# Two of four weight sums per seven-product block moved from VectorE to adding transfers issued from GpSimd, in a two-layer hybrid decoder trunk

## The chip, the cores and the metric

The kernel runs on one core of a Trainium2 chip. A core has five engines that run side by side, each with its own queue: TensorE (PE in the profile; PEld is its loading of weights), VectorE (DVE), ScalarE (ACT), GpSimd (POOL) and SyncE (SP, which here only issues transfers). Waiting is done at the head of an engine's queue, so an instruction that waits holds back all that stand behind it on that engine. The metric is the device time of one execution in microseconds (us).

## The reference, cut to what matters

Two layers of a decoder trunk over 528 positions (16 learned ones and 512 real ones), width 1024. Each layer is an attention part and a feed-forward part:

```python
hn = rmsnorm(h, ffn_norm_g)
ff = jax.nn.silu(jnp.einsum('bld,df->blf', hn, w_gate)) * jnp.einsum('bld,df->blf', hn, w_up)
return h + jnp.einsum('blf,fd->bld', ff, w_down)
```

The change touches only the first two products, with `w_gate` and `w_up`, each 1024 x 2816 in float32. All is held transposed: a tile has 128 features in its partitions and the positions along its free dimension.

## The kernel before

**Products in three parts.** To keep float32 accuracy, each operand is split into a high part (a cast to float32r on ScalarE) and a low part (the rest, by a subtraction on VectorE). A product is then three matmuls: high by high, high by low, low by high. For weights this split is `splits` (line 887: the cast at line 888, the subtraction at line 889); its results lie in two rings of weight buffers, `whi`/`wlo` and `fwhi`/`fwlo`, two buffers each, and successive weight jobs alternate between the rings. A new job's split so waits until TensorE is through with the job four places before it.

**Seven products for eight.** The inner dimension of 1024 is eight blocks of 128. For 19 of the 22 blocks of 128 hidden features (a `Unit`, line 907, f = 3 to 21), gate and up are taken together as a 2 x 2 block product, by a scheme with seven block products in place of eight. It needs sums of weight blocks and sums of input blocks. The input sums are made once per layer by `x_forms` (line 854): four calls, each filling a scratch tile `S` of six parts (lines 861 to 865) and splitting four of them into `th` and `tl`. The weight sums are made per unit: `a` is the block of `w_gate` (tile `raw`, tag with three buffers, shared with the `w_down` loads), `b` the block of `w_up` (tile `fraw`, two buffers), and `s` a further tile with tag `S`, of which there are two buffers in all, shared by `x_forms` and the units. The four sums are those of lines 934, 935, 941 and 947, all on VectorE, each 128 x 512.

**Jobs of a unit.** `make1` splits `a` itself, `make2` builds `s` (lines 934 and 935) and splits it, `make3` overwrites the first half of `b` (line 941) and splits `b`, `make4` overwrites the second half of `a` (line 947) and splits that half. `load` (line 920) issues the two transfers of 512 KB from SyncE. TensorE runs, per unit, `head` (job 1), `middle` (jobs 2 and 3), a group of `w_down` products (line 1035, `down`), `tail` (the rest of job 3, and job 4), and a second group of `down`. `keep` (line 961) and `done` (line 972) bring results out of PSUM: copies at line 966 on ScalarE, sums at lines 969 and 976 on VectorE, then SiLU and the gated product. The first three blocks of hidden features run as plain products (lines 206 and 828 to 849), and during them the four calls of `x_forms` are placed (lines 1236 and 1237).

**Order.** Only TensorE's instructions run in the order written (line 1349). On the other engines the framework sets the order, together with the buffers: an instruction may stand well ahead of its place in the text if it has nothing to wait for. It is fixed when the program is built. The layers share memory: the feed-forward stage's tiles lie on the bytes of the attention stage's tiles and each waits for the users of its own bytes. The next attention stage's first memsets (line 85) are issued from GpSimd in layer 1.

The split of the weights and the loop that calls it ahead:

```python
def need(j):
    for i in range(j, min(j + 3, len(jobs))):
        if i <= j or "make" in jobs[i]:
            convert(i)
```

Of the kernel before, what the change touches and what calls it, by code (L numbers as in the profile page):

```python
# [10 lines left out]
F32 = mybir.dt.float32  # L11
F32R = mybir.dt.float32r
AF = mybir.ActivationFunctionType
ALU = mybir.AluOpType

D = 1024
NK = D // 128
# [3 lines left out]
DEPTH = 2  # L21
# [7 lines left out]
HB = NK // 2  # L29
# [10 lines left out]
def hybrid_kernel(ctx, tc, x_t, w_in, w_fl, w_out, w_gate, w_up, w_down, vecs, b_fg, rope, decay, mask, ident, out_t):  # L40
    nc = tc.nc

    const = ctx.enter_context(tc.tile_pool(name="const", bufs=1))
# [11 lines left out]
    vec = const.tile([128, vecs.shape[1]], F32, name="vec")  # L55
# [70 lines left out]
    def vcol(c):  # L126
        return vec[:, c:c + 1]


    def split(hi, lo, src, pinned=False):  # L130
        pin(nc.scalar.copy(hi, src), pinned)
        pin(nc.vector.tensor_sub(lo, src, hi.bitcast(F32)), pinned)
# [122 lines left out]
    def tt(name, dt=F32):  # L255
        tag, bufs = tags[name]
        return tmp.tile([128, T], dt, name=name, tag=tag, bufs=bufs)
# [4 lines left out]
    def fft(tag, dt=F32R, shape=(128, T), bufs=None):  # L262
        return phase["ffn"].tile(list(shape), dt, name=tag, tag=tag, bufs=bufs)
# [28 lines left out]
    RSC = -1.0 / (2.0 * D)  # L292
# [50 lines left out]
    V_ATTN, V_FFN, V_FIN, V_GN = 0, 2 * NK, 4 * NK, 5 * NK  # L343
# [51 lines left out]
    def silu(t, then=None):  # L395
        nc.scalar.activation(t, t, AF.Silu)
        if then:
            tc.keep_in_program_order(nc.scalar.preload_act_table_set(then))
# [414 lines left out]
    def ffn(l, st, real, last):  # L813
# [8 lines left out]
        def two(t):  # L822
            return t[:, t0:T].rearrange("p (a b) -> p a b", a=2)

        def act_tile(f):
            return fft(f"ah{f % 8}"), fft(f"al{f % 8}")
# [27 lines left out]
        def x_forms(k):  # L854
            def go():
                if k == 0:
                    st["t"] = [[fft(f"t{p}{i}", shape=(128, 2, 4, w)) for p in "hl"] for i in range(2)]
                s = fft("S", F32, (128, 6, w), 2)
                a, b = ((h[k][:, c0:c1], h[HB + k][:, c0:c1]) for c0, c1 in HC)
                g0, g1 = vcol(V_FFN + l * NK + k), vcol(V_FFN + l * NK + HB + k)  # L860
                nc.scalar.activation(s[:, 0:2], two(h[k]), AF.Copy, scale=g0)
                nc.vector.tensor_sub(s[:, 2], s[:, 1], s[:, 0])
                for i in range(2):
                    nc.vector.scalar_tensor_tensor(s[:, 3 + i], b[1], g1, s[:, 1 + i], ALU.mult, ALU.subtract)
                nc.vector.scalar_tensor_tensor(s[:, 5], a[1], g1, s[:, 4], ALU.mult, ALU.subtract)
                th, tl = (t[:, k % 2] for t in st["t"][k // 2])
                split(th, tl, s[:, 2:6])
            return go
# [18 lines left out]
        def splits(hi, lo, src):  # L887
            nc.scalar.copy(hi, src)  # L888
            nc.vector.tensor_sub(lo, src, hi.bitcast(F32))  # L889

        def product(j, o, x, bank, fresh, final, n=HB, done=None):

            def chunk(k):
                def go():
                    if k == 0:
                        need(j)
                    _, hi, lo = jobs[j]["w"][0]
                    xh, xl = x(k)
                    for i, (a, b) in enumerate(((hi, xh), (hi, xl), (lo, xh))):
                        nc.tensor.matmul(bank()[:, 0:b.shape[-1]], a[:, o + k, :], b, start=(fresh and k == 0 and i == 0),  # L900
                                         stop=(k == n - 1 and i == 2), skip_group_check=not (fresh and final))
                    if k == n - 1 and done:
                        done()
                return go
            return [chunk(k) for k in range(n)]

        class Unit:
# [12 lines left out]
            def load(self):  # L920
                if "a" not in self.t:
                    for n, src, pool, tag, bufs in (("a", w_gate, wp, "raw", 3), ("b", w_up, phase["ffn"], "fraw", 2)):
                        self.t[n] = pool.tile([128, NK, 128], F32, name=tag, tag=tag, bufs=bufs)
                        nc.sync.dma_start(self.t[n], src[l, self.f])


            def make1(self, hi, lo):
# [1 line left out]


            def make2(self, hi, lo):
                a, b = self.t["a"], self.t["b"]
                s = self.t["s"] = fft("S", F32, (128, NK, 128), 2)
                nc.vector.tensor_add(s[:, HB:NK], b[:, 0:HB], b[:, HB:NK])
                nc.vector.tensor_sub(s[:, 0:HB], s[:, HB:NK], a[:, 0:HB])
                splits(hi, lo, s)


            def make3(self, hi, lo):
                a, b = self.t["a"], self.t["b"]  # L940
                nc.vector.tensor_sub(b[:, 0:HB], a[:, 0:HB], b[:, 0:HB])
                splits(hi, lo, b)


            def make4(self, hi, lo):
                a, s = self.t["a"], self.t["s"]
                nc.vector.tensor_sub(a[:, HB:NK], a[:, HB:NK], s[:, 0:HB])
                splits(hi, lo, a[:, HB:NK])

            def bank(self, n):  # L950
# [21 lines left out]
            def done(self):  # L972
                e = self.t["e"]
                sg = tt("sg")
                with tc.high_priority():
                    nc.vector.tensor_add(two(sg), self.t["zy"][:, :, 0:w], e[:, 0:2])
                c = slice(t0, T)
                nc.vector.scalar_tensor_tensor(sg[:, c], sg[:, c], RSC, st["R"][:, c], ALU.mult, ALU.mult)
                silu(sg[:, c], None if self.f < NF - 1 else ROOTS if last else LOGS)
                u = tt("tq")  # L980
                nc.vector.scalar_tensor_tensor(u[:, c], sg[:, c], RSC, st["R"][:, c], ALU.mult, ALU.mult)
                u2 = two(u)
                nc.vector.tensor_mul(u2[:, 0], self.t["x"][:, 0:w], u2[:, 0])
                nc.vector.tensor_mul(u2[:, 1], e[:, 2], u2[:, 1])
                fh, fl = act_tile(self.f)
                split(fh[:, c], fl[:, c], u[:, c])
                acts[self.f] = (fh, fl)
# [17 lines left out]
        def down_job(p, f0, f1):  # L1005

            n = f1 - f0
            t = {}

            def load():  # L1010
                if t:
                    return
                t["r"] = wp.tile([128, NK, 128], F32, name="raw", tag="raw", bufs=3)
                for s in range(2):
                    nc.sync.dma_start(t["r"][:, s * n:s * n + n], w_down[l, 2 * p + s, :, f0:f1])

            return add_job(load=load, make=lambda hi, lo: splits(hi, lo, t["r"][:, 0:2 * n]), n=2 * n)
# [31 lines left out]
        for r, (f0, f1) in enumerate(ROUNDS):  # L1049
            for f in range(f0, f1):  # L1050
# [4 lines left out]
                u = Unit(f)  # L1055
# [7 lines left out]
                if fills:  # L1063
                    p, g0, g1 = fills.pop(0)
# [175 lines left out]
        steps.insert(4, lambda: squares(st, QC, False, False))  # L1240
        return steps

    gf = const.tile([128, NK], F32, name="gf")
    nc.vector.tensor_scalar_mul(gf, vec[:, V_FIN:V_FIN + NK], RSC)

    def layer(l):
# [79 lines left out]
        for g in range(2):  # L1326
# [15 lines left out]
                      ret_places(3, 52, 45.5, 47.5, 57.5, 55.5, 58.5, 60, 64.1, 63, 64.2))  # L1342
        plan += [op[3], op[7], op[11], op[15]] + op[16:]
        up = ffn(l, ff, real, real)
        plan += [lambda: enter("ffn"), start_ffn] + up
        return plan
# [77 lines left out]
```

## Time and profile before

| | |
|---|---|
| Median of 3 runs | 1272.61 us (1271.99 to 1272.77) |
| The profiled execution's own time | 1272.43 us |
| Its span | 1270.6 us |
| PE busy | 1253.3 us |
| DVE busy | 998.6 us |
| ACT busy | 687.3 us |
| POOL busy | 266.9 us |
| Granted clock of TensorE, mean | 0.999 |
| Transferred | 120.57 MB, mean 95 GB/s |

The profile shows one execution of the program. Times on its time line count from the start of the span. A group's row gives line, engine, operation, result <- operands, shape and count, then busy time and mean duration in ns, then the idle time of the engine before these instructions and what ended it. A row of the time line gives start, duration, engine, line and operation, and in brackets the idle time ahead of it with its releaser. A row of the waits gives total, number and longest. Transfers have a time from issue to landing.

### The profile page before, as it was taken

What the parts mean: (1) busy time and instruction counts of PE and PEld (TensorE: products, weight loads), DVE (VectorE), ACT (ScalarE), POOL (GpSimd) and SP (SyncE); (2) the same over time, 40 slices, a digit from 0 to 9 for tenths busy, and PEclk for the clock granted to TensorE, in tenths of its full rate; (3) what the DMA queues carried; (4) which work ended last, traced back from release to release, by engine and by line L of the source; (5) the groups of instructions that cost most, each with busy time, mean ns of one, the idle gap of its engine ahead of it and who ended that gap; (6) DMA issues with size and microseconds to landing.
All of it is one profiled execution on the core that took longest, in us unless ns stands there. A gap on an engine that the chain in (4) does not pass through costs nothing.

```text
span 1270.6 us, 23600 instructions
## 1 busy us (share of the span) xinstructions
PE 1253.3 (99%) x9263; PEld 1195.1 (94%) x9263; DVE 998.6 (79%) x1852; ACT 687.3 (54%) x1246; POOL 266.9 (21%) x527
## 2 busy tenths in 40 slices
PE   9999999999999999999999999999999999999997
PEld 8899999999999999999998989998789999999996
DVE  8878756779888888887786877567899888888866
ACT  7666545676444444444465665456764444444444
POOL 3455545410000000000025546454100000000000
PEclk9999999999999999999999999999999999999999
DMA  6322222123233333332323232222233333333321
GB/s 217 95 71 89 87 81 83 60 68 129 92 96 100 100 100 100 100 100 84 107 70 117 61 101 83 78 90 67 100 96 121 100 100 100 100 100 100 102 81 67
DMA packets 45680, 120.57 MB, mean 95 GB/s; under 512 B 5360, under 2 KB 12272, under 8 KB 45568
## 3 DMA queue, kind: packets, MB, share of 16 engines
q1 hardware_dynamic: 45136, 118.77, 29.7%
q8 instruction: 73, 1.20, 0.4%
q14 instruction: 39, 0.32, 0.1%
q10 hardware_dynamic: 432, 0.29, 0.1%
HBM read 116.91 MB, written 2.13 MB: 94 GB/s over the span
## 4 chain that ended last, share of the span: by engine, by line
PE 93%; DVE 2%; ACT 2%; DMA 2%; issue 0%; SPq 0%; DVEq 0%; ACTq 0%
PE psd L206 29%; PE psa L900 19%; PE psd L1035 14%; PE psd L900 13%; PE psa L206 5%; PE psa L1035 4%; PE psa L407 2%; PE psa L582 2%; PE psa L497 2%; PE psa L749 1%; PE psa L719 1%; DMA bc<-cdr 1%; DMA h<-x_t 0%; DMA cdr<-z 0%; PE psa L279 0%
## 5 line engine op out<-in xcount | busy, mean ns | idle before, releaser
L183 POOL TENSOR_TENSOR wlo<-raw,whi 128x128 fp32r<-128x128 f32 x504 | 261.4, 554 | 270.0 <-ACT whi L180 250.0
L206 PE MATMUL psd<-xh,whi 128*128 128x264 f32 (+1 forms) x792 | 195.4, 314 | 0.2 <-ACT whi L180 0.2
L206 PE MATMUL psd<-xl,whi 128*128 128x264 f32 (+1 forms) x792 | 186.0, 302 | 0.5 <-DVE xl L309 0.4
L206 PE MATMUL psd<-xh,wlo 128*128 128x264 f32 (+1 forms) x792 | 186.4, 303 | 0.0
L206 PEld LDWEIGHTS psd<-xh,whi 128*128 128x128 f32 x792 | 128.0, 189 | 5.2 <-ACT whi L180 0.9
L206 PEld LDWEIGHTS psd<-xh,wlo 128*128 128x128 f32 x792 | 126.8, 188 | 6.3 <-DVE wlo L183 0.6
L206 PEld LDWEIGHTS psd<-xl,whi 128*128 128x128 f32 x792 | 127.4, 188 | 5.0 <-DVE xl L309 1.2
L180 ACT CAST whi<-raw 128x512 fp32r<-128x512 f32 (+1 forms) x168 | 98.4, 613 | 49.3 <-PE psd L206 36.4
L888 ACT CAST whi<-raw 128x1024 fp32r<-128x1024 f32 (+2 forms) x62 | 54.8, 885 | 51.3 <-PE psd L900 39.9
L888 ACT CAST fwhi<-raw 128x1024 fp32r<-128x1024 f32 (+2 forms) x62 | 55.6, 897 | 47.5 <-PE psd L900 40.0
L1135 POOL TENSOR_TENSOR th<-th,e 128x544 f32<-128x544 f32 x1 | 1.4, 1370 | 359.1 <-DVE e L1155 359.1
L85 POOL MEMSET kl<- 64x528 f32 x2 | 1.1, 534 | 345.4 <-PE psa L900 345.4
L889 DVE TENSOR_TENSOR wlo<-raw,whi 128x1024 fp32r<-128x1024 f32 (+2 forms) x62 | 62.9, 1015 | 12.8 <-ACT whi L888 12.7
L889 DVE TENSOR_TENSOR fwlo<-raw,fwhi 128x1024 fp32r<-128x1024 f32 (+2 forms) x62 | 64.0, 1032 | 10.5 <-ACT fwhi L888 10.1
L900 PE MATMUL psa<-th,whi 128*128 128x264 f32 (+1 forms) x232 | 65.4, 282 | 0.0
L900 PE MATMUL psa<-th,wlo 128*128 128x264 f32 (+1 forms) x232 | 65.4, 282 | 0.0
L900 PE MATMUL psa<-tl,whi 128*128 128x264 f32 (+1 forms) x232 | 65.3, 282 | 0.0
L900 PE MATMUL psa<-th,fwhi 128*128 128x264 f32 (+1 forms) x224 | 63.4, 283 | 0.0
L900 PE MATMUL psa<-tl,fwhi 128*128 128x264 f32 (+1 forms) x224 | 63.3, 283 | 0.0
L900 PE MATMUL psa<-th,fwlo 128*128 128x264 f32 (+1 forms) x224 | 63.3, 282 | 0.0
L517 ACT ACTIVATE pd<-pd,nmax 128x144 f32<-128x144 f32 (+1 forms) x64 | 36.9, 576 | 43.8 <-DVE nmax L504 31.8
L966 ACT COPY e<-psa 128x264 f32<-128x264 f32 (+1 forms) x114 | 42.9, 376 | 28.4 <-PE psa L900 24.1
(343 smaller groups left out, 4053.5 us busy)
## 6 DMA issues: line engine op xcount, KB each, us to landing
raw<-w_in SPq DMA_DIRECT2D x54, 512.0 KB, 3.4
raw<-w_gate SPq DMA_DIRECT2D x44, 512.0 KB, 3.8
fraw<-w_up SPq DMA_DIRECT2D x38, 512.0 KB, 3.5
raw<-w_down SPq DMA_DIRECT2D x64, 256.0 KB, 2.8
raw<-w_out SPq DMA_DIRECT2D x16, 512.0 KB, 3.4
raw<-w_down SPq DMA_DIRECT2D x32, 192.0 KB, 2.5
bc<-cdr SPq DMA_DIRECT2D x16, 264.0 KB, 3.5
raw<-w_up SPq DMA_DIRECT2D x6, 512.0 KB, 3.5
```

The costliest lines, as they stand in the source:

```text
L180: pin(nc.scalar.copy(hi, job["raw"][:, c0:c1]), pinned)
L183: pin(sub(lo[:, i:i + wide], job["raw"][:, c0 + i:c0 + i + wide], hi[:, i:i + wide].bitcast(F32)), pinned)
L206: nc.tensor.matmul(ps[1][b][:, 0:c1 - c0], w[:, wk, :], x[:, c0:c1], start=(k == 0 and i == 0), stop=(k == n - 1 and i == 2))
L407: nc.tensor.transpose(ps[:, 128 * j:128 * j + 128], src[:, o:o + 128], idt)
L497: nc.tensor.matmul(sc[0:nq, 0:c1 - c0], st["q"][s][:, q0:q0 + nq], kk[:, c0:c1], start=(i == 0), stop=(i == 1))
L517: nc.scalar.activation(pr, pr, AF.Exp, bias=nmax[0:nq], scale=-1.0, accum_out=rsum)
L582: nc.tensor.matmul(po[:, c0:SEQ], v[:, j, :], pp[:, j, META + c0:T], start=(j == 0 and i == 0), stop=(j == 4 and i == 1))
L888: nc.scalar.copy(hi, src)
L889: nc.vector.tensor_sub(lo, src, hi.bitcast(F32))
L900: nc.tensor.matmul(bank()[:, 0:b.shape[-1]], a[:, o + k, :], b, start=(fresh and k == 0 and i == 0), stop=(k == n - 1 and i == 2), skip_gr ...
L966: nc.scalar.copy(self.t["e"][:, i], self.t["x"][:, 0:w])
L1035: nc.tensor.matmul(v[:, 0:c1 - c0], a[:, s * n + k, :], b[:, c0:c1], start=(k == 0 and i == 0), stop=(k == n - 1 and i == 2))
```

## The change

In `x_forms` the order of subtractions is turned so that some parts change sign; two of them now use a negated norm weight, from a new tile `ngf` made at the start. In `load`, the tile `s` is taken at once: its second half is loaded with the first half of the `w_up` block (a plain transfer of 256 KB from SyncE), and a transfer issued from GpSimd adds the second half of the `w_up` block to it. A further transfer from GpSimd adds the first half of the `w_gate` block to the first half of `b`. `make2` and `make3` lose the sums of lines 934 and 941; the two sums that stay become additions. A sign in `done` makes up for the turned signs.

```diff
                 g0, g1 = vcol(V_FFN + l * NK + k), vcol(V_FFN + l * NK + HB + k)
+                n1 = ngf[:, l * HB + k:l * HB + k + 1]
                 nc.scalar.activation(s[:, 0:2], two(h[k]), AF.Copy, scale=g0)
-                nc.vector.tensor_sub(s[:, 2], s[:, 1], s[:, 0])
-                for i in range(2):
-                    nc.vector.scalar_tensor_tensor(s[:, 3 + i], b[1], g1, s[:, 1 + i], ALU.mult, ALU.subtract)
-                nc.vector.scalar_tensor_tensor(s[:, 5], a[1], g1, s[:, 4], ALU.mult, ALU.subtract)
+                nc.vector.tensor_sub(s[:, 2], s[:, 0], s[:, 1])
+                nc.vector.scalar_tensor_tensor(s[:, 3], b[1], g1, s[:, 1], ALU.mult, ALU.subtract)
+                nc.vector.scalar_tensor_tensor(s[:, 4], b[1], n1, s[:, 2], ALU.mult, ALU.subtract)
+                nc.vector.scalar_tensor_tensor(s[:, 5], a[1], n1, s[:, 4], ALU.mult, ALU.subtract)
...
                         nc.sync.dma_start(self.t[n], src[l, self.f])
+                    s = self.t["s"] = fft("S", F32, (128, NK, 128), 2)
+                    nc.sync.dma_start(s[:, HB:NK], w_up[l, self.f, :, 0:HB])
+                    nc.gpsimd.dma_start(s[:, HB:NK], w_up[l, self.f, :, HB:NK], accum_op=ALU.add)
+                    nc.gpsimd.dma_start(self.t["b"][:, 0:HB], w_gate[l, self.f, :, 0:HB], accum_op=ALU.add)
...
             def make2(self, hi, lo):
-                a, b = self.t["a"], self.t["b"]
-                s = self.t["s"] = fft("S", F32, (128, NK, 128), 2)
-                nc.vector.tensor_add(s[:, HB:NK], b[:, 0:HB], b[:, HB:NK])
-                nc.vector.tensor_sub(s[:, 0:HB], s[:, HB:NK], a[:, 0:HB])
+                a, s = self.t["a"], self.t["s"]
+                nc.vector.tensor_add(s[:, 0:HB], s[:, HB:NK], a[:, 0:HB])
                 splits(hi, lo, s)
...
             def make3(self, hi, lo):
-                a, b = self.t["a"], self.t["b"]
-                nc.vector.tensor_sub(b[:, 0:HB], a[:, 0:HB], b[:, 0:HB])
-                splits(hi, lo, b)
+                splits(hi, lo, self.t["b"])
...
             def make4(self, hi, lo):
                 a, s = self.t["a"], self.t["s"]
-                nc.vector.tensor_sub(a[:, HB:NK], a[:, HB:NK], s[:, 0:HB])
+                nc.vector.tensor_add(a[:, HB:NK], a[:, HB:NK], s[:, 0:HB])
...
-                nc.vector.scalar_tensor_tensor(u[:, c], sg[:, c], RSC, st["R"][:, c], ALU.mult, ALU.mult)
+                nc.vector.scalar_tensor_tensor(u[:, c], sg[:, c], -RSC, st["R"][:, c], ALU.mult, ALU.mult)
...
+    ngf = const.tile([128, DEPTH * HB], F32, name="ngf")
+    for i in range(DEPTH):
+        c = V_FFN + i * NK + HB
+        nc.vector.tensor_scalar_mul(ngf[:, i * HB:i * HB + HB], vec[:, c:c + HB], -1.0)
```

## The prediction

> **What bounds the kernel now.** First the page: span, busy time, the chain that ended last.
>
> ```profile
> span 1270.6 us, 23600 instructions
> ...
> PE 1253.3 (99%) x9263; PEld 1195.1 (94%) x9263; DVE 998.6 (79%) x1852; ACT 687.3 (54%) x1246; POOL 266.9 (21%) x527
> ...
> PE 93%; DVE 2%; ACT 2%; DMA 2%; issue 0%; SPq 0%; DVEq 0%; ACTq 0%
> ```
>
> TensorE carries 93% of the chain and is idle for 1270.6 - 1253.3 = 17.3 us in all. VectorE is next at 79%. The change takes work from VectorE, so the second question is whether VectorE ever ends a wait of TensorE in the feed-forward stage, where all of the change lies. The view by windows answers for one stretch in which the stage has just begun (300 to 310 us) and one well inside it; after the length come the busy times of PE, PEld, DVE, ACT and POOL, the granted clock, the DMA share and GB/s.
>
> ```profile
> 300.00:310.00 10.00, 10.00 (x85) 10.00 (x84) 10.00 (x20) 6.53 (x10) 0.00 (x0) 1.00 0.15 52
> 400.00:500.00 100.00, 100.00 (x826) 100.00 (x825) 80.28 (x119) 45.04 (x64) 0.00 (x0) 1.00 0.33 105
> ```
>
> TensorE is busy for all of both, at full clock, although VectorE is full in the first and at 80% in the second. The view of TensorE's own waits has no row at all from 264 to 646 us, and from 960 us on only one at the very end (line 1159). So a faster VectorE has nothing to give here; what matters is how much slack each result has. The chain in one unit of layer 0:
>
> ```profile
> 500.12 2.92 PE psa L1035 x24
> ...
> 511.81 1.45 PE psa L900 x12
> ```
> ```profile
> 516.16 2.92 PE psa L1035 x24
> ```
>
> A unit repeats every 516.16 - 500.12 = 16.04 us, at 2.92 / 24 = 0.122 us per matmul. At 511.81 TensorE begins the unit's second weight job (the one that reads S).
>
> **The change part by part.** Removed from VectorE are two sums per unit:
>
> ```profile
> L934 DVE TENSOR_TENSOR S<-fraw 128x512 f32<-128x512 f32 x38 | 26.3, 691 | 23.3 <-DMA fraw<-w_up 23.3
> ```
> ```profile
> L941 DVE TENSOR_TENSOR fraw<-raw,fraw 128x512 f32<-128x512 f32 x38 | 26.0, 684 | 0.0
> ```
>
> That is 38 x (0.691 + 0.684) = 52.3 us of busy time and 23.3 us of waits for w_up, out of 998.6. None of it is on the path: in steady state VectorE already idles a fifth of the time. Saved at the end: 0.
>
> Subtractions that become additions, the two sums that stay (lines 935, 947), the four of x_forms and the sign in `done` keep form and count: 0. New are two small VectorE products for the negated norm weights, at the start of the program:
>
> ```profile
> 4.43 0.77 DVE L309 SCALAR_TENSOR_TENSOR xl<-h,vec,xh 128x528 fp32r<-128x528 f32 x1 [0.42 <-ACT xh L308]
> ```
> ```profile
> L784 DVE TENSOR_SCALAR gn<-vec x8: 121/144/154, 3.8 to 778.4; 128x1 f32<-128x1 f32 x8
> ```
>
> At about 0.14 us each they fit into the 0.42 us for which VectorE waits before 4.43. Without that cover they would cost 0.3 us.
>
> Added for each unit are one plain load of 256 KB (SyncE) and two adding transfers of 256 KB (GpSimd). The load has rows of its size, and the a block has one of its own; the adding transfer has none. Then w_up's spread of landing times:
>
> ```profile
> raw<-w_gate SPq DMA_DIRECT2D x44, 512.0 KB, 3.8
> ```
> ```profile
> raw<-w_down SPq DMA_DIRECT2D x64, 256.0 KB, 2.8
> ```
> ```profile
> DMA to landing us min/median/max: 3.3/3.5/5.0
> ```
>
> An adding transfer cannot land sooner than a plain one of its size (2.8 us), since it moves the same bytes and also reads what it adds to. I bound it above by two of the slowest landings of 512 KB, 10.0 us, and take 2 x 2.8 = 5.6 us, as it reads two streams of 256 KB. "DMA: Bandwidth & Descriptors" of the Trainium skill, section "Anatomy of one DMA — SWDGE (gpsimd) path", fits transfers issued from GpSimd as about 2.0 us plus bytes / 436e3, which gives an estimate of 2.6 us for 256 KB; no run here shows it, and with it the sum would be the same.
>
> Does the longer sequence load, add, sum stay hidden? SyncE's queue, then VectorE and ScalarE on the same unit's tiles:
>
> ```profile
> 492.51 0.80 SPq L1015 DMA_DIRECT2D raw<-w_down  x2
> 494.95 0.33 SPq L924 DMA_DIRECT2D fraw<-w_up  x1
> 497.09 0.33 SPq L924 DMA_DIRECT2D raw<-w_gate  x1
> ```
> ```profile
> 498.48 0.69 DVE L934 TENSOR_TENSOR S<-fraw 128x512 f32<-128x512 f32 x1 [0.72 <-DMA fraw<-w_up]
> ```
> ```profile
> 501.79 0.69 DVE L935 TENSOR_TENSOR S<-S,raw 128x512 f32<-128x512 f32 x1
> ```
> ```profile
> 505.54 1.23 DVE L889 TENSOR_TENSOR fwlo<-S,fwhi 128x1024 fp32r<-128x1024 f32 x1 [1.78 <-ACT fwhi L888]
> ```
> ```profile
> 504.46 1.05 ACT L888 CAST fwhi<-S 128x1024 fp32r<-128x1024 f32 x1 [3.92 <-PE psa L900]
> ```
>
> The split at 504.46 is of the unit before: its weight buffer came free only then. So the S built at 498 to 502 is split one period later, at 504.46 + 16.04 = 520.5. Its buffer's previous user ended its split one period before 505.54 + 1.23 = 506.77, at 490.7, so the new load can go as early as that, ahead of w_down, or at the latest behind w_gate at 497.4. It lands at 493.5 or 500.2, the adding transfer at 499.1 or 505.8 (with the 10.0 us bound at 510.2). Line 935 stands at 501.79 and also needs w_gate, which lands at 497.09 + 3.8 = 500.9. So it is on time in the early order and about 4 us late in the late one, still 14 us before 520.5. The second adding transfer has the whole 16 us: b is split later still.
>
> The wait is taken at the head of VectorE's queue. Behind line 935 stand the evacuations of line 1040 and the low half at 505.54, which ends at 506.77 and is used at 511.81: 5.0 us of slack. A hold of 4 us fits; the 8.4 us of the far bound would cost 3.4 us in a unit. I take the middle value: 0. SyncE pays 0.33 us per load in a queue that mostly waits.
>
> GpSimd is idle in this stage, but its queue is not empty:
>
> ```profile
> POOL th L1135 <- DVE e L1155: 359.1, 1, 359.1
> POOL kl L85 <- PE psa L900: 345.4, 1, 345.4
> ```
>
> The memset of line 85 waits for 345.4 us until the stage's products are done, and line 1135 likewise in layer 1. The adding transfers must stand ahead of both, since those products need them. They delay nothing there: 0. The traffic grows by 768 KB per 16.04 us, about 49 GB/s beside 105; with the extra read the share goes from 0.33 to at most 0.33 x (105 + 49 + 33) / 105 = 0.59, so loads land a little later, inside the slack above.
>
> What remains is the entry of the stage, where S is also the scratch of x_forms (two buffers for all):
>
> ```profile
> 286.22 0.90 SPq L924 DMA_DIRECT2D fraw<-w_up  x2
> ```
> ```profile
> 287.54 0.74 ACT L861 ACTIVATE S<-h,vec 128x528 f32<-128x528 f32 x1
> ```
> ```profile
> 315.70 1.25 DVE L132 TENSOR_TENSOR tl<-S,th 128x1056 fp32r<-128x1056 f32 x1
> ```
> ```profile
> 320.43 1.22 DVE L889 TENSOR_TENSOR fwlo<-S,fwhi 128x1024 fp32r<-128x1024 f32 x1
> ```
> ```profile
> 324.97 0.28 PE L900 MATMUL psa<-th,fwhi 128*128 128x264 f32 x1
> ```
>
> Both first w_up loads go at 286.22, 29 us ahead of their use, as soon as their bytes are free; a load of S will do the same and keep a buffer from about 287 until 320.43 + 1.22 = 321.65. Then x_forms 1 to 3 go through the other buffer one after another. The view of tile S gives min/median/max in ns for each step of one of them:
>
> ```profile
> L864 DVE SCALAR_TENSOR_TENSOR S<-h,vec,S x16: 475/483/490, 294.4 to 939.8; 128x264 f32<-128x264 f32 x8, 128x256 f32<-128x256 f32 x8
> L861 ACT ACTIVATE S<-h,vec x8: 709/726/739, 287.5 to 929.0; 128x528 f32<-128x528 f32 x4, 128x512 f32<-128x512 f32 x4
> L862 DVE TENSOR_TENSOR S<-S x8: 415/422/428, 294.0 to 933.3; 128x264 f32<-128x264 f32 x4, 128x256 f32<-128x256 f32 x4
> L865 DVE SCALAR_TENSOR_TENSOR S<-h,vec,S x8: 475/485/494, 295.8 to 940.8; 128x264 f32<-128x264 f32 x4, 128x256 f32<-128x256 f32 x4
> L131 ACT CAST th<-S x8: 1037/1058/1077, 296.8 to 941.3; 128x1056 fp32r<-128x1056 f32 x4, 128x1024 fp32r<-128x1024 f32 x4
> L132 DVE TENSOR_TENSOR tl<-S,th x8: 1217/1240/1260, 297.9 to 942.4; 128x1056 fp32r<-128x1056 f32 x4, 128x1024 fp32r<-128x1024 f32 x4
> ```
>
> One takes 0.73 + 0.42 + 2 x 0.48 + 0.49 + 1.06 + 1.24 = 4.9 us in a row. The last ends now at 315.70 + 1.25 = 316.95; with one buffer I put it one such time later, at 321.9. TensorE needs it nine matmuls after 324.97, at 326.06. It fits with 4 us to spare: 0.
>
> **The sum** is 0 on the profiled execution's 1272.43 us (span 1270.6 and 1.83 around it). The median of the runs is 1272.61, 0.18 higher; I forecast that median, 1272.6.
>
> **Rivals.** *Both S buffers taken at the entry.* If the loads of units 3 and 4 both get a buffer before x_forms are through, the remaining ones wait until 321.65. With n of them left the last ends at 321.65 + 4.9 n against 326.06: 0.5 us late for one, 5.4 for two, 10.3 for three. It decides from two on. For it speaks that these loads have no other condition; against it that the first x_form (287.54) is ready about as early as the loads, and that the 4.9 us were to be had only once. Two left in one layer gives 1272.6 + 5.4 = 1278, in both 1283.4.
>
> *GpSimd held up beside a full VectorE.* Its transfers are set up by the engine itself. The next rows are GpSimd's subtractions of line 183 and VectorE's first idle moment after 283 us.
>
> ```profile
> L183 POOL TENSOR_TENSOR wlo<-raw,whi x504: 447/463/2073, 21.5 to 897.7; 128x128 fp32r<-128x128 f32 x168
> ```
> ```profile
> 329.07 1.23 DVE L889 TENSOR_TENSOR fwlo<-raw,fwhi 128x1024 fp32r<-128x1024 f32 x1 [0.32 <-ACT fwhi L888]
> ```
>
> Some of those subtractions took 2073 ns instead of 463. If setting up had to wait for a gap in VectorE, the first adding transfer would start at 328.75, land at 334.35, and after the sum (0.69) and the cast (1.05) the weights would be there at 336.1 instead of 324.97: 11.1 us, 1283.7; in both layers 1294.8. It decides once S is added later than about 323. Against it: the median is near the minimum. "SBUF — State Buffer" of the Trainium skill, section "Who interferes with whom", supports the mechanism for two-port copies of VectorE but excludes a two-input tensor_tensor for descriptor writing, as an inference; the rows here cannot show which.
>
> *Faster.* TensorE's 17.3 idle us lie outside this stage. Only a shifted order of the queues in layer 1's attention could give some back; I put 3 us on it, 1269.5.
>
> *The change does not do what it says*: VectorE would wait at line 935 for the adding transfer as it did at line 934 for w_up (23.3 us). The busy time goes, the wait stays. Same time; it is part of the forecast.
>
> **How the numbers follow.** Forecast 0.52, buffers taken 0.22, GpSimd held up 0.18, faster 0.08. About 0.2% (2.5 us) is what a measurement of this kernel can tell from no change; the forecast's own range is 1270.3 to 1275.0. Same is 0.52, slower 0.22 + 0.18 = 0.40, faster 0.08. The range runs from 1270.3 (leaving out faster) to 1287, which leaves out the second rival in both layers, some 0.1.
>
> **What would show it.** Right: the two groups of lines 934 and 941 are gone, VectorE's busy time is near 998.6 - 52 = 946, TensorE has no waits inside the stage, and a unit still repeats every 16.04 us. A TensorE wait for th or tl at the first unit means the first rival; a wait for weights from S there, with the adding transfer landing late, the second. A period above 16.04 us would mean that adding transfers land later than my 10.0 us and VectorE's queue is held in each unit. Wrong altogether would be a gain inside the stage.

## The result and the profile after

The changed kernel takes 1280.29 us (median of 4 runs, 1278.02 to 1281.75) against 1272.33 us before (4 runs, 1271.99 to 1272.77): a ratio of 1.0058, 95% interval 1.0044 to 1.0071. It became slower by 0.6%. Most lines of `Unit` stand one further down in it: the last sum is line 948 (was 947), the evacuations of h, which bring it out of PSUM, are lines 1041 and 1043 (were 1040 and 1042). The loads are lines 925 to 929, and the sum into S that stays is line 938 (was 935). The page of the profiled execution (1278.02 us) has the span, the busy times and the shares of the chain:

```profile
span 1276.2 us, 23833 instructions
...
PE 1255.2 (98%) x9263; PEld 1195.7 (94%) x9263; DVE 953.3 (75%) x1778; ACT 686.6 (54%) x1246; POOL 332.7 (26%) x603
...
PE 90%; DVE 4%; DMA 3%; ACT 2%; issue 1%; DVEq 0%; SPq 0%; ACTq 0%
```

VectorE has lost 998.6 - 953.3 = 45.3 us of work, and yet VectorE and transfers have gained 3 points of the chain. The view by windows (columns as in the prediction) and the chain show the middle of layer 0:

```profile
400.00:500.00 100.00, 100.00 (x825) 100.00 (x825) 74.29 (x109) 45.45 (x65) 11.21 (x13) 1.00 0.56 150
```
```profile
503.36 2.92 PE psa L1036 x24
...
519.39 2.92 PE psa L1036 x24
```

There nothing is lost: TensorE is full, and a unit repeats every 16.03 us as before. So I cut the chain into four stretches, at the same four instructions in each kernel. After, they are these rows (a place in layer 0 ahead of the feed-forward part, the first products behind that part, a place in layer 1 ahead of its own, the last row of the program):

```profile
275.91 4.13 PE psd L206 x34
...
647.71 4.84 PE psd L206 x21
...
928.37 5.30 PE psa L206 x23
...
1271.43 1.13 DVE tl L1136 x2
```

Before, they begin at 275.09, 644.47, 925.57 and 1266.05. The differences, and the same for every later run:

| kernel | to the first mark | layer 0 | between | layer 1 |
|---|---|---|---|---|
| before | 275.09 | 369.38 | 281.10 | 340.48 |
| after | 275.91 | 371.80 | 280.66 | 343.06 |
| e1_signs | 275.25 | 369.37 | 280.21 | 340.50 |
| e2_b_add | 275.76 | 369.37 | 280.12 | 340.49 |
| e3_s_add | 276.39 | 372.18 | 280.24 | 346.20 |
| e4_entry | 275.10 | 369.37 | 280.05 | 340.49 |
| e5_pin | 276.25 | 372.80 | 280.24 | 343.89 |
| e6_plain | 275.17 | 369.54 | 280.08 | 342.01 |
| e7_first | 275.84 | 369.38 | 280.45 | 342.28 |
| e8_third | 275.58 | 370.94 | 282.23 | 341.28 |
| e9_pin5 | 275.17 | 370.33 | 280.39 | 342.62 |
| e10_pool | 275.60 | 371.89 | 280.58 | 345.51 |
| e11_again | 275.47 | 371.63 | 280.67 | 347.19 |

Layer 0 costs 2.42 us and layer 1 2.58 us more. (The 282.23 of e8 is a matter of the clock, in the last section.) In both layers TensorE's own waits are new and lie at the entry, most of them while the third block that is made of seven products (f = 5) is being prepared. The view of TensorE's waits (us in total, times, longest):

```profile
PE psd L1036 <- DVE h L1043: 2.3, 1, 2.3
...
PE psa L901 <- ACT e L967: 1.0, 2, 0.7
```

What VectorE does at layer 0's entry, from its time line, before and then after (start, duration, line; in brackets the idle time ahead and what ended it):

```profile
318.62 0.68 DVE L935 TENSOR_TENSOR S<-S,raw 128x512 f32<-128x512 f32 x1
319.22 0.68 DVE L941 TENSOR_TENSOR fraw<-raw,fraw 128x512 f32<-128x512 f32 x1
319.82 0.68 DVE L947 TENSOR_TENSOR raw<-raw,S 128x512 f32<-128x512 f32 x1
...
326.87 0.68 DVE L889 TENSOR_TENSOR wlo<-raw,whi 128x512 fp32r<-128x512 f32 x1
...
331.15 0.68 DVE L935 TENSOR_TENSOR S<-S,raw 128x512 f32<-128x512 f32 x1
```
```profile
320.41 0.69 DVE L938 TENSOR_TENSOR S<-S,raw 128x512 f32<-128x512 f32 x1 [2.41 <-DMA S<-w_up]
...
329.34 0.68 DVE L890 TENSOR_TENSOR wlo<-raw,whi 128x512 fp32r<-128x512 f32 x1
...
336.81 0.69 DVE L938 TENSOR_TENSOR S<-S,raw 128x512 f32<-128x512 f32 x1 [4.43 <-DMA raw<-w_gate]
337.42 0.76 DVE L1041 TENSOR_TENSOR h<-psa,h 128x264 f32<-128x264 f32 x2
```

And SyncE's loads, before and after:

```profile
324.41 0.33 SPq L924 DMA_DIRECT2D fraw<-w_up  x1
327.58 0.33 SPq L924 DMA_DIRECT2D raw<-w_gate  x1
```
```profile
312.56 0.33 SPq L927 DMA_DIRECT2D S<-w_up  x1
...
328.83 0.33 SPq L925 DMA_DIRECT2D fraw<-w_up  x1
330.05 0.33 SPq L925 DMA_DIRECT2D raw<-w_gate  x1
```

The chain reads so. The first S load goes out only at 312.56, when an `x_forms` call has freed an S buffer. A plain transfer and then an adding one follow each other, and VectorE waits 2.41 us at line 938. All of VectorE's work behind it is later. The last sum of this first block (line 948, was 947) comes at 324.24 instead of 319.82. The low half of that sum is the last to read the block's w_gate buffer; its cast stands on ScalarE behind the cast of the last plain block's result, which is late too, and so it starts at 329.34 instead of 326.87. So the buffer is free later: the third block's w_gate is issued at 330.05 instead of 327.58, now only 1.2 us behind w_up instead of 3.2, and takes 6.67 us to land (3.4 before), as the chain has it:

```profile
330.05 6.67 DMA raw<-w_gate
...
342.41 1.74 PE psa L901 x12
345.61 1.72 PE psa L901 x12
```

At 332.4 VectorE arrives at the third block's line 938 and stands there for 4.43 us, and behind it stand the evacuations that TensorE needs. TensorE's gaps in this entry come to 1.4 us, of which 0.34 us lie ahead of that hold, at 329.18, in a wait for e behind ScalarE's late casts. Another part of layer 0's 2.42 us is that some rows of 12 matmuls take 1.73 us, as the last two do, where they take 1.45 otherwise. In layer 1 the same place waits for the adding transfer itself, as the chain has it:

```profile
955.66 7.74 DMA S<-w_up
...
963.42 0.04 DVE S L938
...
964.77 2.33 PE psd L1036 x9
```

The wait of 2.25 us and the row of 2.33 us, which took 2.06 before, are 2.5 of the 2.58 us. The transfers' own times, from the page of after (KB each, median us from issue to landing):

```profile
fraw<-w_gate POOLq DMA_DIRECT2D x38, 256.0 KB, 4.1
...
S<-w_up POOLq DMA_DIRECT2D x38, 256.0 KB, 4.7
```

### The profile page after: what moved, and what is told of

Its sections match the earlier page's. It is cut to its first block, busy times and chain, and to the rows that moved or that the text cites. A ratio compares the mean times of both kernels' runs of the same rounds, so it can differ in the third digit from the quotient of the medians.

```text
span 1276.2 us, 23833 instructions
## 1 busy us (share of the span) xinstructions
PE 1255.2 (98%) x9263; PEld 1195.7 (94%) x9263; DVE 953.3 (75%) x1778; ACT 686.6 (54%) x1246; POOL 332.7 (26%) x603
## 4 chain that ended last, share of the span: by engine, by line
PE 90%; DVE 4%; DMA 3%; ACT 2%; issue 1%; DVEq 0%; SPq 0%; ACTq 0%
PE psd L206 28%; PE psa L901 18%; PE psd L1036 14%; PE psd L901 12%; PE psa L206 5%; PE psa L1036 4%; PE psa L407 2%; PE psa L582 2%; PE psa L497 2%; PE psa L749 1%; PE psa L719 1%; DMA S<-w_up 1%; DMA raw<-w_gate 1%; DMA bc<-cdr 1%; DMA h<-x_t 0%
## 5 line engine op out<-in xcount | busy, mean ns | idle before, releaser
L928 POOL DMA_DIRECT2D S<-w_up x38 | 32.8, 863 | 326.3 <-DVE h L1043 238.3
L929 POOL DMA_DIRECT2D fraw<-w_gate x38 | 33.0, 867 | 224.0 <-DMA fraw<-w_up 131.3
L889 ACT CAST fwhi<-S 128x1024 fp32r<-128x1024 f32 x20 | 21.0, 1049 | 71.3 <-PE psa L901 66.3
```

Source lines behind the costliest of these rows:

```text
L928: nc.gpsimd.dma_start(s[:, HB:NK], w_up[l, self.f, :, HB:NK], accum_op=ALU.add)
L929: nc.gpsimd.dma_start(self.t["b"][:, 0:HB], w_gate[l, self.f, :, 0:HB], accum_op=ALU.add)
```

## The experiments

Three theories stood at the start. T1: at each layer's entry line 938 waits for late data while evacuations stand behind it on VectorE. T2: the added traffic slows loads all along. T3: the turned signs, `ngf` or the new `x_forms` cost it. Their predictions differ most where parts of the change are taken out.

**e1_signs**: only the signs.

```diff
-  (the S load and both GpSimd transfers)
+  nc.vector.tensor_add(s[:, HB:NK], b[:, 0:HB], b[:, HB:NK])    # in make2
+  nc.vector.tensor_add(b[:, 0:HB], a[:, 0:HB], b[:, 0:HB])      # in make3
```

> Only the moved signs: all four weight sums stay on VectorE (as additions), no transfer is issued from GpSimd, ngf and the new x_forms stand. T1 (at each layer's entry the S sum of the third block waits for a late landing with evacuations queued behind it) and T2 (the added traffic slows loads all along) both expect the time of the kernel before, 1272.3 us within 1. T3 (the signs, ngf or the new x_forms cost it) expects about 1280.

Measured 1272.49 us, ratio 1.0005 (0.9996 to 1.0014). T3 is out.

**e2_b_add** and **e3_s_add**: one adding transfer each.

```diff
 e2, in load and make2:
-  nc.gpsimd.dma_start(s[:, HB:NK], w_up[l, self.f, :, HB:NK], accum_op=ALU.add)
+  nc.vector.tensor_add(s[:, HB:NK], s[:, HB:NK], b[:, HB:NK])
 e3, in load and make3:
-  nc.gpsimd.dma_start(self.t["b"][:, 0:HB], w_gate[l, self.f, :, 0:HB], accum_op=ALU.add)
+  nc.vector.tensor_add(b[:, 0:HB], a[:, 0:HB], b[:, 0:HB])
```

> S's second half is loaded plain by SyncE and its sum is made on VectorE again; the only adding transfer left is w_gate into the w_up tile. T1: the GpSimd half of the late S is gone, so layer 1's entry is repaired (its third block waited for S) and layer 0's is not necessarily (its third block waited for w_gate): 1273 to 1277. T2: half of the adding transfers, about half of the loss: 1276.

> Only the adding transfer into S is left; the first half of the w_up tile is summed on VectorE again. T1: the S sum still waits at both entries: 1277 to 1280. T2: about half of the loss: 1276.

e2 took 1273.20 us, 1.0008 (1.0000 to 1.0017), in T1's range; e3 took 1280.57 us, 1.0064 (1.0051 to 1.0077), just above it. Both carry 38 adding transfers of 256 KB; one has nearly none of the loss and the other all of it. Traffic by itself (T2) does not explain that. The early plain load of S does no harm either: e2 has it, and the third block's sum stands unwaited on VectorE's time line of e2 (the sum ahead of it waited 1.93 us for w_up, which cost nothing):

```profile
332.30 0.68 DVE L938 TENSOR_TENSOR S<-S,raw 128x512 f32<-128x512 f32 x1
```

What is left is the second transfer on top of the first, into S.

**e4_entry**: the first three blocks of each layer as before, all later ones as after.

```diff
+  if self.f < 6: return                     # in load, ahead of the S load
+  if self.f < 6: (the sums of make2 and make3 on VectorE)
```

> The first three blocks of each layer make their sums on VectorE and load no S early; all later blocks have both adding transfers as in the kernel after. T1: the entries run as in the kernel before, 1272.5 to 1273.5. T2: 19 of 25 or so blocks keep the added traffic, so most of the loss stays: 1278 to 1279.

Measured 1272.60 us, 1.0002 (0.9993 to 1.0011). With 32 of 38 blocks still using both adding transfers (16 of 19 in a layer, not the 19 of 25 or so of the expectation), the whole loss is gone, and both layers have their old length to 0.01 us (table). T1 holds as to the place. T2 is out.

**e7_first** and **e8_third**: only the first, or only the third block as before (`self.f == 3`, `self.f == 5` in place of `self.f < 6`).

> Only the first seven-product block of each layer (f = 3) makes its sums on VectorE and loads no S early; all others as after. If the third block's wait is inherited (first block's late S, hence its raw buffer free late, hence the third w_gate issued late): the third w_gate is issued near 327.6 us instead of 330.05 and the time is 1272.5 to 1275. If the third block's own adding transfer is what is late: 1277 to 1281.

> Only the third seven-product block of each layer (f = 5) makes its sums on VectorE; the first two load and add as after. If the wait is inherited from the first block, the third w_gate still goes out near 330 us and layer 0 keeps most of its 2.4 us, while layer 1, whose third block waited for S itself, loses its wait: 1275 to 1278. If the third block's own transfers are the cause: 1272.5 to 1274.

e7 took 1274.71 us, 1.0019 (1.0010 to 1.0028). SyncE's time line of e7:

```profile
327.79 0.33 SPq L925 DMA_DIRECT2D raw<-w_gate  x1
```

The third w_gate is on time again, though it was the first block that was changed, and layer 0 has its old length (369.38). The third block's sum still waits 0.94 us for it, which costs nothing. So in layer 0 the loss comes with the first block's delay. Layer 1 keeps 1.80 us, since there the third block's own adding transfer is late; e7's chain:

```profile
952.95 7.01 DMA S<-w_up
```

e8 took 1275.26 us, 1.0027 (1.0016 to 1.0038): layer 0 keeps 1.56 us, with the third w_gate issued at 330.06, and layer 1 only 0.80. Both times lie in the ranges expected for an inherited wait, but in layer 0 e8's trace shows another wait than the one that was meant. The third block's sum no longer waits, although w_gate was issued as late: it landed in 4.9 us instead of 6.67, with no adding transfers of its own block beside it. What stays is TensorE's wait for e ahead of it, which after has too. VectorE's row and TensorE's:

```profile
335.02 0.69 DVE L944 TENSOR_TENSOR S<-S,raw 128x512 f32<-128x512 f32 x1
```
```profile
329.19 0.39 PE L901 MATMUL psa<-th,whi 128*128 128x264 f32 x1 [0.71 <-ACT e L976]
```

So the hold at the third block of layer 0 took both, the w_gate that the first block made late and the third block's own transfers. In layer 1 the third block's transfers cost the more. Only e4, which leaves both out, removes the loss.

**e5_pin** and **e9_pin5**: the order on VectorE.

```diff
 e5:
-  nc.vector.tensor_add(s[:, 0:HB], s[:, HB:NK], a[:, 0:HB])
+  pin(nc.vector.tensor_add(s[:, 0:HB], s[:, HB:NK], a[:, 0:HB]))
 e9: the same, but only if self.f == 5
```

> As the kernel after, but the S sum (line 938) keeps its place in the written order on VectorE, so that it cannot stand ahead of the evacuations. T1a (the loss is the evacuations queued behind a sum that waits; the weights themselves come in time): 1272.5 to 1275, and TensorE no longer waits for h at line 1043 or e at line 967. T1b (the weights themselves come too late for their products): TensorE waits for splits or weights instead, 1277 to 1281.

e5 missed both numbers: 1283.55 us, 1.0084 (1.0072 to 1.0097). The waits for h and e are gone as expected, but the written place of the first block's sum lies behind an evacuation that ends the plain products. VectorE's time line of e5:

```profile
323.42 0.71 DVE L844 SCALAR_TENSOR_TENSOR tq<-psd,R 128x528 f32<-128x528 f32 x1 [3.67 <-PE psd L206]
...
326.61 0.68 DVE L938 TENSOR_TENSOR S<-S,raw 128x512 f32<-128x512 f32 x1
```

Its split follows, and TensorE, which has gone through the first block's job 1, waits for both parts of it:

```profile
328.43 0.40 PE L901 MATMUL psa<-th,fwhi 128*128 128x264 f32 x1 [2.15 <-ACT fwhi L889]
...
329.69 0.39 PE L901 MATMUL psa<-th,fwlo 128*128 128x264 f32 x1 [0.75 <-DVE fwlo L890]
```

The pin had moved a first-block sum that was in time behind something late, so e5 says nothing on the third block. e9 pins that one alone.

> As the kernel after, but in the third block of each layer (f = 5) alone the S sum keeps its written place on VectorE, behind the evacuations of h and e. All transfers are the same and as late. T1a (the loss is the evacuations queued behind the sum that waits): TensorE's waits for h at line 1043 and e at line 967 go, 1273 to 1276. T1b (the third block's weights themselves come too late for their products): TensorE waits for the splits of S instead, 1277 to 1281.

e9 took 1275.17 us, 1.0022 (1.0013 to 1.0031), of which layer 0 has 0.95 us left and layer 1 2.14. The third w_gate was as late as ever (issued 329.64), but VectorE went on with h while it was on its way:

```profile
332.61 0.77 DVE L1043 TENSOR_TENSOR h<-psa,h 128x264 f32<-128x264 f32 x2 [0.63 <-PE psa L1038]
```

So much of the loss was not late weights, but what stood behind the wait for them (T1a): by the medians 2.8 us are left of some 8, by the profiles 3.1 of 5.0 (after) or 9.0 (e11). TensorE's waits for h are gone; those for e are not, against the expectation. What is left is only partly traced: short waits of TensorE for e (1.5 us in three) behind casts that ScalarE does later, and the fourth block's line 938 in layer 1, not pinned, waiting 1.70 us for w_gate.

**e6_plain**: is it the adding, or the second transfer?

```diff
-  nc.gpsimd.dma_start(..., accum_op=ALU.add)    # both
+  nc.gpsimd.dma_start(...)
```

> Both GpSimd transfers are plain instead of adding; this leaves two of the four weight sums out, and nothing else differs. If adding is what makes these transfers slow: the 256 KB of S land in about 2.6 us as from SyncE, not 4.7, the S sum waits some 2 us less at each entry, and the time falls to 1273 to 1276. If the second of two serial transfers (plain, then on top of it), however made, is what is late: 1278 to 1281 as after.

Measured 1274.53 us, 1.0016 (1.0007 to 1.0025). From the page of e6:

```profile
fraw<-w_gate POOLq DMA_DIRECT2D x38, 256.0 KB, 3.0
...
S<-w_up POOLq DMA_DIRECT2D x38, 256.0 KB, 3.6
```

The time fell as expected for slow adding, with less at hand than expected: plain, the transfers land in 3.6 and 3.0 us instead of 4.7 and 4.1, so adding costs 1.1 us each, not 2.1. With 1.1 us less in each block the wait in layer 0 nearly vanishes (369.54), in layer 1 1.5 us stay.

**e10_pool**: is it SyncE's queue, in which w_up and w_gate stand behind a load that waits for an S buffer?

```diff
-  nc.sync.dma_start(s[:, HB:NK], w_up[l, self.f, :, 0:HB])
+  nc.gpsimd.dma_start(s[:, HB:NK], w_up[l, self.f, :, 0:HB])
```

> The plain half of S is issued by GpSimd too, ahead of the adding transfer, so that SyncE's queue never waits for an S buffer and the third w_up and w_gate are issued when their own buffers come free. If the loads behind SyncE's wait are what is late: 1273 to 1276, with the third w_up issued near 325 us instead of 328.8. If the late S of the first blocks holds the w_gate buffers anyway: 1278 to 1281 as after.

It came out between the two, 1276.53 us, 1.0035 (1.0023 to 1.0047). On SyncE's time line of e10 the third w_up goes out at 327.90 (after: 328.83) and the third w_gate at 330.52 (after: 330.05). With no S load ahead of them they are about as late as in after, so they wait for their buffers, not for SyncE. Why the median is nevertheless 3 to 4 us lower than after's is not settled: the profiled execution has both layers at least as long as after, but at 1280.05 us it is the slowest of the five (the others: 1274.55 to 1276.91).

**e11_again**: the kernel after once more.

> The kernel after once more, unchanged, for a second profile: the median of its runs is 8 us above before, its first profile only 5.6. The layer-0 stage should again be 2 to 3 us longer than before and the layer-1 stage 2.5 to 6; the rest of the program, the wait for the first loads included, should stand within 1 us of before.

Measured 1279.50 us, 1.0054 (1.0041 to 1.0068). Layer 0 came as expected (+2.25); layer 1 did not, with +6.71. Here the third block's line 938 in layer 1 waits longer, and for w_gate, where in the first profile it waited for the adding transfer. Its row on VectorE's time line, the view by windows (the three last columns are the granted clock, the DMA share and GB/s) and the chain of e11_again:

```profile
964.53 0.69 DVE L938 TENSOR_TENSOR S<-S,raw 128x512 f32<-128x512 f32 x1 [5.06 <-DMA raw<-w_gate]
```
```profile
964.00:966.00 2.00, 0.12 (x1) 0.12 (x1) 1.47 (x3) 0.00 (x0) 0.00 (x0) 0.62 0.16 28
966.00:968.00 2.00, 2.00 (x5) 1.62 (x6) 2.00 (x3) 0.00 (x0) 0.00 (x0) 0.50 0.06 6
```
```profile
965.88 4.21 PE psd L1036 x9
970.09 2.02 PE psa L901 x12
```

The granted clock fell to 0.50 while TensorE waited 3.3 us. Before, at full clock, the same two rows are:

```profile
959.74 2.06 PE psd L1035 x9
961.80 1.42 PE psa L900 x12
```

That is 6.23 - 3.48 = 2.75 us on top of the wait. In the first profile of after the wait was 2.3 us and the clock stayed at 1.00. The two profiles of this one kernel differ mainly there: the wait in layer 1 varies from run to run, and in the longer case the clock fell as well. The other executions have no trace, so it is not shown that all of the distance between the median's 8 us and the first profile's 5.6 lies there.

## Why the prediction was wrong, step by step

- **The removed sums are worth 0: right.** e1 keeps them, e4 is rid of 64 of the 76, and neither differs from before by a measurable amount. Their busy time was mis-sized: 45.3 us instead of 52.3. In the rows of before, three sums of 0.68 us start 0.60 us apart, and 76 x 0.60 = 45.6.
- **Signs, `ngf`: 0, right** (e1).
- **The adding transfer, 5.6 us: near.** Measured 4.7 and 4.1 us, at the longest 7.7, inside the bounds of 2.8 and 10.0. The Trainium skill's fit ("DMA: Bandwidth & Descriptors", section "Anatomy of one DMA — SWDGE (gpsimd) path") gives an estimate of 2.6 us; even plain the transfers took 3.6 and 3.0 here.
- **Steady state hidden: right.** 16.03 us a unit, and e4 has no loss with 32 blocks in it.
- **GpSimd's queue and rival two, GpSimd held up beside a full VectorE: not seen.** Each of its issues took 0.86 us (0.853 to 0.881 for S), also those at the entry. The symptom that I had put beside this rival, S late at the first units, did occur, but through the buffer and the two transfers in a row.
- **Rival four, the wait goes from line 934 to the sum behind it: came about in size.** Line 938 waits 19.9 us in all (7.6 for S, 12.3 for w_gate) where line 934 waited 23.3. That this costs nothing held in the steady state, not at the entry.
- **Rival one, both S buffers taken at the entry: did not occur**, as the load of S was not issued early.
- **The step that failed is the entry of the stage.** I wrote that "a load of S will do the same and keep a buffer from about 287", and then asked only whether `x_forms` would still be in time. The load went at 312.56 instead, and it was the block itself that came late; the term that I put at 0 there measured 2.42 us in layer 0 and 2.58 in layer 1. With a load behind an `x_forms` call my own terms would have shown it: 312.56, which is known only afterwards, + 2.8 + 5.6 = 321.0 against line 935 at 318.62, 2.4 us. That the wait was 2.41 is luck: the two transfers took 7.8 us, not 8.4, and VectorE stood ready at 318.0. I had worked out the late order for the steady state alone, and at the entry only the early one.
- **"A hold of 4 us fits"** came from 5.0 us of slack in the steady state. At the third block the hold was 4.43 us (layer 0) and TensorE waited for e, with VectorE's and ScalarE's queue in between; in layer 1 it was 4.01 us and TensorE waited 2.3 us for h. What stands behind line 938 at the entry is not what stands there later.
- **The range held** (1270.3 to 1287.0), since the rivals put late weights at the entry inside it; the forecast of no change did not hold.

## What to carry to other kernels

A step that is hidden in the steady state must be priced once more at the stage's entry, where its buffers still belong to the stage before and no period of slack has built up; do it for both orders of the loads. On an engine that works in order, a sum that waits costs what stands behind it, so look for that rather than for the sum's own due time. Replacing an instruction that had everything at hand by a second transfer on top of a first trades 0.6 us of an idle engine for 4 to 5 us of latency.

## What the runs showed of the hardware that was not expected

**The clock can fall after a short wait.** At the third block of layer 1, TensorE idle for 2.3 us (after) kept 1.00; with 2.6 us (e3), 3.2 us (e10) and 3.3 us (e11) the granted clock went to 0.50 for some microseconds. The view of TensorE's waits and that by windows of e3:

```profile
PE psd L1037 <- DVE h L1044: 2.6, 1, 2.6
```
```profile
968.00:970.00 2.00, 2.00 (x6) 1.54 (x6) 1.99 (x3) 0.38 (x1) 0.00 (x0) 0.50 0.35 126
```

The length of the wait alone does not decide it. In layer 1's attention the kernels have a gap of 1.5 to 1.8 us (line 407); before, with 1.80 us, kept 1.00, and in e8, with 1.80 us too, the clock fell behind it. e8's stretch between the layers is the longest of all (282.23). The view by windows of e8:

```profile
682.00:684.00 2.00, 2.00 (x8) 1.74 (x7) 1.54 (x6) 0.72 (x2) 0.00 (x0) 0.50 0.57 207
```

"TensorE: Matmul & The Clock Gate" of the Trainium skill, section "HAM oscillation — how this bites in real kernels", warns of idle gaps beyond about 3.4 us. The halving agrees; the length does not, as 2.6 us were enough in e3 and 1.8 us in e8.

**An adding transfer loads the DMA engines twice.** The software queue of after and of e6 moved the same bytes (packets, MB, share of 16 engines):

```profile
q0 software_dynamic: 10944, 19.93, 10.2%
```
```profile
q0 software_dynamic: 6080, 19.93, 5.1%
```

Adding took 1.8 times the packets and twice the time of the engines. GpSimd's own part, from the view of the line in after and in e6 (ns, min/median/max):

```profile
L928 POOL DMA_DIRECT2D S<-w_up x38: 853/862/881, 315.6 to 1196.6; - x38
```
```profile
L928 POOL DMA_DIRECT2D S<-w_up x38: 536/536/538, 314.9 to 1191.5; - x38
```

An issue that adds holds GpSimd for 0.86 us, a plain one for 0.54.

**Left open**: the first mark lies anywhere from 275.09 to 276.39 us. It varies between two runs of one kernel too (275.91 and 275.47 for after), and none of the kernels was made to settle it.
